# First stage of a two-layer trunk written as an explicit in-order pipeline on four queues

## The chip, the cores and the metric

The kernel runs on 1 core of one Trainium2 chip. The metric is the device time of one execution in microseconds (us), taken as the median of the runs of a kernel. Below, PE is TensorE, DVE is VectorE, ACT is ScalarE, POOL is GpSimd, and SP is SyncE, whose queue issues nearly all transfers.

## The reference

One sequence of 512 tokens with model width 2048 goes through two layers. Layer 0 is forgetting attention (32 heads of 64), layer 1 is RWKV-7 time mixing; each sits under a normalisation whose shift and scale come from a second input `c`, and ends in a gated residual addition. Everything is float32. What matters here is the head of layer 0:

```python
c_act = jax.nn.silu(c)                                  # (1, 2048)
mod = c_act @ w_mod[i] + b_mod[i]                       # 3 * 2048 outputs
shift, scale, gate = jnp.split(mod, 3, axis=-1)
h = rms_norm(x, norm_w[i]) * (1.0 + scale) + shift      # (512, 2048)
# layer 0:
proj = h @ w_in                                         # 2048 -> 4 * 2048 + 32
q, k, v, z, f_logit = ...                               # parts of proj
out = (softmax(q k / 8 + cum_t - cum_s) v * silu(z)) @ w_out
```

## The kernel before

Activations are held transposed, as 16 tiles of 128 channels by 512 tokens (`KT = 16`). A product in float32 quality is made of three matmuls on operands cut into a high and a low half (`mm3`): high weight by high activation, low weight by high activation, high weight by low activation. So each weight tile is loaded (`raw`), copied by ACT into its high half (`whi`), and DVE subtracts to get the low half (`wlo`). Activations are cut likewise (`hi`, `lo`).

The first stage (the block `with tc.tile_pool(name="st0"...)`, from line 397) does this. The tiles of x are loaded, squared and summed over channels on PE (`ss`); from that comes the reciprocal root `rstd`. `cb` is silu(c) spread over all partitions. `mod_unit` makes shift or scale for one channel tile: it loads a 128 x 2048 tile of w_mod in two halves (`wm`, 512 KB each), DVE multiplies each by `cb` and sums along the row into one column of `mraw`, and POOL adds the two columns and the bias (for scale also multiplies by the norm weight). Then, for each k of 16: the stage's weights `wst0` (672 columns: forget gates and q, k, v of the first heads) are loaded and cut; `xn` is x by `rstd` on POOL (DVE for k = 0), shift and scale are put on by ACT, the result is cut into `A[k]`; and six products go into six PSUM banks (`tr`, `pv`, `ss`, `tr`, `S`, `S`), each accumulated over the 16 k. After k = 3, 7 and 11 come nine blocks of the gate projection z (`NZ = 9`): for each of nine output tiles a 256 KB weight tile is loaded and cut, twelve matmuls run into one of two `pj` banks, ACT copies the bank to `zt`, and POOL adds it to `zs` (the first time ACT writes `zs` itself). The last quarter of these nine tiles is made later (`zfin`).

All of this stage's program order on each engine is chosen by a scheduler from the dependences. Buffers come in rings: three `wm`, three `raw`, four `whi`, four `wlo`; a load waits until the ring's oldest tile has had its last reader. SP takes its transfers strictly in order.

After the stage the order is written out by a planner (`Flow` and `backbone`): a list of weight tiles is multiplied in a fixed row on PE, with the side work of attention (normalisation of q and k in `norm`, scores, transposes) placed in between at planned times. `InOrder.on` forces each engine to keep the order in which instructions are written; it is switched on there for PE, ACT and DVE. The first four weight tiles are fetched and cut ahead of the first product, then `first()` starts the side work: ACT copies k of the first heads out of PSUM, squares q for its norm, and so on.

Of the kernel before, what the change touches and what calls it, by code (L numbers as in the profile page):

```python
# [17 lines left out]
P = 128  # L18
T = 512
# [110 lines left out]
def body(ctx, tc, a, out, dbg=None, stop=0):  # L130
# [258 lines left out]
    with ExitStack() as s0:  # L389
# [7 lines left out]
        with tc.tile_pool(name="st0", bufs=2, reuse_waits="tile") as q:  # L397
            xs = []
            cb, cs, i = silu_c(cbp)
            s0.enter_context(table("natural_log_exp_and_others", i))  # L400
            for k in range(KT):
                x = q.tile([P, T], F, tag=f"r{k}", name=f"x{k}", bufs=1)
                sp.dma_start(x, a["xT"][k])
                xs.append(x)
            ss = bank("ss")
            for k in range(KT):
                sq = q.tile([P, T], F, tag=("sq", "sq", "xn", "zt")[k % 4], name="sq",
                            bufs=4 - k % 4 // 2 * 2)
                if k < 5:
# [3 lines left out]
                if k % 2:  # L413
                    dve.tensor_tensor(out=sq, in0=old, in1=sq, op=OP.add)
                    pe.matmul(ss, onesD, sq, start=k == 1, stop=k == KT - 1)
                if k % 2 and k < 8:
                    o = bank("tr")
                    for i in range(4):
                        n = k // 2 * 4 + i
                        pe.matmul(o[:, i * P:(i + 1) * P], cs[:, n:n + 1].broadcast_to([P, P]),  # L420
                                  ident, start=True, stop=True)
                    act.activation(cb[:, k // 2 * T:(k // 2 + 1) * T], o, AF.Copy)
                old = sq
            rstd = rstd_of(q, ss, eps, 1e-6, "rs0", bufs=1)
            st = [bank(t) for t in ("tr", "pv", "ss", "tr", "S", "S")]
            cols = [(0, P)] + [(32 + i * P, 32 + (i + 1) * P) for i in range(5)]
            for k in range(KT):
                for part in (1, 0):
                    for _ in mod_unit(q, cb, 0, part, k):
                        pass  # L430
                w = wload(a["wst0"][k:k + 1].rearrange("k p n -> p k n"), 1, NS0, "s", q)
                xn = q.tile([P, T], F, tag="xn", name="xn")
                (pool if k else dve).tensor_tensor(out=xn, in0=xs[k], in1=rstd, op=OP.mult)
                act.activation(xn, xn, AF.Identity, scale=scale[:, 0, k:k + 1],
                               bias=shift[:, 0, k:k + 1])
                A.append(new_act(k))
                split(A[k][0], A[k][1], xn)
                for o, (m0, m1) in zip(st, cols):
                    mm3(o[0:m1 - m0, :], w, 0, A[k], k == 0, k == KT - 1, m0, m1)
                if k % WK < WK - 1 or k == KT - 1:  # L440
                    continue
                k0 = k - WK + 1
                for j in range(NZ):
                    w = wload(a["wz"][j][:, k0:k + 1, :], WK, P)
                    o = bank("pj")
                    for i in range(WK):
                        mm3(o, w, i, A[k0 + i], i == 0, i == WK - 1)
                    if k0 == 0:
                        act.activation(zs[j], o, AF.Copy)
# [258 lines left out]
        def gatings():  # L708
            while len(odone) < KT or len(mdone) < 12 * KT:
# [905 lines left out]
```

## Time and profile before

| | |
|---|---|
| median of 3 runs | 2509.62 us (2505.53 to 2510.38) |
| the profiled execution | 2509.14 us |
| its span, first to last instruction | 2507.4 us |
| mean granted PE clock | 0.973 |
| PE busy | 2350.3 us, 94%, 13620 matmuls |
| DVE busy | 1659.4 us, 66% |
| ACT busy | 1251.2 us, 50% |
| POOL busy | 864.4 us, 34% |
| transfers | 476.08 MB, mean 190 GB/s |

A busy share is an average over stages with different limits. In the table of 40 slices the PE row begins `6878999`, so the first slices, about 62.7 us each, are less full than most others. All helpers record their operations under one line (L88), so instructions are told apart by the names of their tiles. A matmul's recorded duration is longer than its distance to the next one, since matmuls overlap; the distance is the pace.

### The profile page before, as it was taken

How to read it: one execution, taken by the hardware profiler on the slowest of the kernel's cores; microseconds unless marked ns; L12 is line 12 of the kernel's file. 1: busy time of each engine (PE TensorE's matmuls, PEld its weight loads, DVE VectorE, ACT ScalarE, POOL GpSimd, SP SyncE). 2: the span in 40 equal slices, each digit the busy share in tenths (PEclk: the TensorE clock that was granted, in tenths of full speed). 3: DMA queues.
4: the chain of work that ended last, by engine and by line, in shares of the span. 5: the costliest groups of instructions: out<-in, count | busy, mean ns of one | idle time of the engine just before them, and what ended most of it. 6: DMA issues, size and time to landing. Idle time of an engine off the chain costs nothing. (4 is left out here: it accounts for less than half of the span.)

```text
span 2507.4 us, 40113 instructions
## 1 busy us (share of the span) xinstructions
PE 2350.3 (94%) x13620; PEld 1818.3 (73%) x13620; DVE 1659.4 (66%) x3143; ACT 1251.2 (50%) x2300; POOL 864.4 (34%) x1280
## 2 busy tenths in 40 slices
PE   6878999999999999996999998997999999999999
PEld 4666777877777788884766676776677767777787
DVE  6776878888887545339696666662567877776332
ACT  3335655555565544226447775742344545555321
POOL 4464533433333100117341239731334444442000
PEclk8989999999999999998999998998999999999999
DMA  8765666666664264445656886776756656554443
GB/s 277 259 236 174 213 208 202 214 207 209 208 212 153 93 230 164 144 135 184 205 168 230 279 250 206 224 212 193 195 159 176 191 157 179 161 149 149 147 147 97
DMA packets 343582, 476.08 MB, mean 190 GB/s; under 512 B 146768, under 2 KB 157136, under 8 KB 343376
## 3 DMA queue, kind: packets, MB, share of 16 engines
q1 hardware_dynamic: 341712, 470.88, 60.5%
q0 software_dynamic: 1664, 2.63, 0.3%
q8 instruction: 108, 1.77, 0.3%
q14 instruction: 98, 0.80, 0.1%
HBM read 377.42 MB, written 95.95 MB: 189 GB/s over the span
## 5 line engine op out<-in xcount | busy, mean ns | idle before, releaser
L88 PE MATMUL pj<-hi,whi 128*128 128x512 f32 x2416 | 995.4, 412 | 31.1 <-ACT zt L88 13.1
L88 PE MATMUL pj<-hi,wlo 128*128 128x512 f32 x2416 | 958.3, 397 | 14.0 <-DVE wlo L88 13.9
L88 PE MATMUL pj<-lo,whi 128*128 128x512 f32 x2416 | 957.7, 396 | 2.3 <-DVE lo L88 2.3
L88 DVE TENSOR_TENSOR wlo<-raw,whi 128x512 fp32r<-128x512 f32 (+2 forms) x628 | 488.0, 785 | 288.9 <-ACT whi L88 284.9
L88 ACT ACTIVATE whi<-raw 128x512 fp32r<-128x512 f32 (+2 forms) x628 | 394.0, 634 | 421.9 <-PE pj L88 229.5
L88 PEld LDWEIGHTS pj<-hi,whi 128*128 128x128 f32 x2416 | 459.8, 190 | 139.5 <-ACT zt L88 15.7
L88 PEld LDWEIGHTS pj<-lo,whi 128*128 128x128 f32 x2416 | 459.6, 190 | 106.2 <-DVE lo L88 3.4
L88 PEld LDWEIGHTS pj<-hi,wlo 128*128 128x128 f32 x2416 | 460.9, 191 | 102.5 <-DVE wlo L88 18.4
L88 DVE CUSTOM_DVE_ANT_0 wm<-wm,cb 128x1024 f32<-128x1024 f32 x192 | 245.4, 1285 | 23.7 <-DMA wm<-in_wmodT 23.5
L88 POOL TENSOR_SCALAR SV<-SV,dec 64x64 f32<-64x64 f32 x224 | 92.4, 413 | 220.1 <-DVE SV L88 205.7
L88 POOL TENSOR_SCALAR mx<-mx 128x1 f32<-128x1 f32 x128 | 64.8, 507 | 144.3 <-DVE mx L88 96.6
L88 ACT ACTIVATE pr<-Sm,mx 128x128 f32<-128x128 f32 (+3 forms) x128 | 71.5, 559 | 80.2 <-POOL mx L88 80.1
L88 POOL TENSOR_SCALAR pr<-pr,rc 128x128 f32<-128x128 f32 (+3 forms) x128 | 97.0, 758 | 22.6 <-DVE rc L88 18.4
L88 DVE COPY SV<-x 64x64 f32<-64x64 f32 x256 | 56.7, 222 | 62.7 <-PE x L88 55.6
L88 DVE CUSTOM_DVE_ANT_0 Sm<-S,cmask 128x128 f32<-128x128 f32 (+3 forms) x128 | 62.1, 485 | 34.6 <-PE S L88 33.7
L88 POOL TENSOR_TENSOR lt<-lane 128x30 f32<-128x30 f32 (+14 forms) x90 | 61.9, 687 | 64.3 <-DMA lane<-mld 57.5
L88 POOL TENSOR_TENSOR acc<-acc,sq 128x512 f32<-128x512 f32 x14 | 18.2, 1297 | 161.5 <-ACT sq L88 161.5
L88 DVE TENSOR_TENSOR SV<-SV,x 64x64 f32<-64x64 f32 x224 | 49.0, 219 | 37.5 <-PE x L88 31.9
L88 POOL TENSOR_SCALAR scale<-mraw,bsc 128x1 f32<-128x1 f32 x32 | 39.8, 1244 | 97.9 <-DVE mraw L88 96.6
L88 POOL TENSOR_TENSOR lane<-lane,lt 128x30 f32<-128x30 f32 (+14 forms) x90 | 63.6, 706 | 7.0
L88 POOL TENSOR_TENSOR bk<-bk,eI 128x512 f32<-128x512 f32 x32 | 36.8, 1151 | 79.4 <-PE S L88 53.4
L88 PE MATMUL S<-k,q 128*128 128x128 f32 (+7 forms) x256 | 62.4, 325 | 0.0
(316 smaller groups left out, 3478.3 us busy)
## 6 DMA issues: line engine op xcount, KB each, us to landing
wm<-in_wmodT SPq DMA_DIRECT2D x192, 512.0 KB, 4.5
raw<-in_wz SPq DMA_DIRECT2D x128, 256.0 KB, 3.8
raw<-in_wo SPq DMA_DIRECT2D x128, 256.0 KB, 3.6
raw<-in_wv SPq DMA_DIRECT2D x124, 256.0 KB, 3.7
raw<-in_wk SPq DMA_DIRECT2D x96, 256.0 KB, 3.6
raw<-in_wr SPq DMA_DIRECT2D x64, 256.0 KB, 4.6
raw<-in_wq SPq DMA_DIRECT2D x56, 256.0 KB, 3.9
mxd<-m SPq DMA_DIRECT2D x48, 256.0 KB, 3.0
```

The costliest lines, as they stand in the source:

```text
L88: self.last = f(*a, **k)
```

## The change

The four queues PE, ACT, DVE and SP are switched to the written order for the first stage, and the stage is written out as a pipeline in that order.

- w_mod tiles are loaded whole (1 MB; only the first two in halves), three in the ring, and `mod0` reduces one with a single instruction. The bias is the start value of the sum, and the result is written to `shift` or `scale` directly. The norm weight enters in the operation that makes `xn`. POOL does nothing in the stage.
- The squares of the first six x tiles go to `ss` singly instead of in pairs; `cb` is made before the squares that ACT does.
- The products of z are spread over the steps: `z_unit` is one k of one z tile (three matmuls). For k below 4 two tiles advance by one unit per step; later a step has 7 units (k below 8) or 9 between the products of the stage's own columns. Weights of z are loaded four tiles ahead (`z_load`) and cut two ahead (`z_split`).
- ACT copies the first quarter of each z tile out of PSUM as before; the additions of the second and third are done by DVE straight from PSUM (`zadds`).
- In step k the operand of step k + 1 is made after the first third of the products, and two w_mod tiles are reduced after the second and the last third.
- The condition in `gatings` counts 8 KT instead of 12 KT reductions, because `mod0` does not enter its reductions in `mdone`.

```diff
-            for k in range(KT):
+            for e in (pe, act, dve, sp):
+                e.on = True
...
+            def mod0(n, parts=1):
+                if n >= 2 * KT:
+                    return
+                k, part, w, m = n // 2, 1 - n % 2, wms[n], D // parts
+                acc = (bsc[:, 0, k:k + 1] if part else vecs[:, V_BM, k:k + 1])
+                for i in range(parts):
+                    s = slice(i * m, (i + 1) * m)
+                    o = (scale if part else shift)[:, 0, k:k + 1] if i == parts - 1 else \
+                        mraw[:, part, i:i + 1]
+                    dve.tensor_tensor_reduce(out=w[:, s], in0=w[:, s], in1=cb[:, s], scale=1.0,
+                                             scalar=acc, op0=OP.mult, op1=OP.add, accum_out=o)
+                    acc = o
...
+            def operand(k):
+
+                if k >= KT:
+                    return
+                xn = q.tile([P, T], F, tag="xn", name="xn")
+                dve.scalar_tensor_tensor(out=xn, in0=xs[k], scalar=vecs[:, V_NW, k:k + 1],
+                                         in1=rstd, op0=OP.mult, op1=OP.mult)
+                act.activation(xn, xn, AF.Identity, scale=scale[:, 0, k:k + 1],
+                               bias=shift[:, 0, k:k + 1])
+                A.append(new_act(k))
+                act_hi(A[k][0], xn)
+                dve.tensor_tensor(out=ws[k][1], in0=rws[k], in1=ws[k][0], op=OP.subtract)
+                zadds()
+                dve.tensor_tensor(out=A[k][1], in0=xn, in1=A[k][0], op=OP.subtract)
...
+            def z_unit(n, i):
+                j, g = zt[n]
+                if i == 0:
+                    zo[n] = bank("pj")
+                mm3(zo[n], zw[n], i, A[g * WK + i], i == 0, i == WK - 1)
+                if i == WK - 1:
+                    zend.append(n)
+
+            def zadds():
+                while zend:
+                    n = zend.pop(0)
+                    j, g = zt[n]
+                    if g == 0:
+                        act.activation(zs[j], zo.pop(n), AF.Copy)
+                    else:
+                        dve.tensor_tensor(out=zs[j], in0=zs[j], in1=zo.pop(n), op=OP.add)
...
+                if k == 11:
+                    mod0(0, 2)
...
+            mod0(1, 2)
...
+            w_hi(0)
+            operand(0)
+            w_load(1)
+            wm_load(3)
+            wm_load(4)
+            for n in range(2):
+                z_split(n)
+            mod0(2)
+            mod0(3)
...
             for k in range(KT):
-                for part in (1, 0):
-                    for _ in mod_unit(q, cb, 0, part, k):
-                        pass
...
+                w_hi(k + 1)
+                for part in range(3):
+                    for o, (m0, m1) in list(zip(st, cols))[2 * part:2 * part + 2]:
+                        mm3(o[0:m1 - m0, :], ws[k], 0, A[k], k == 0, k == KT - 1, m0, m1)
+                    if k < WK:
+                        if part:
+                            z_unit(part - 1, k)
                     else:
-                        z = q.tile([P, T], F, tag="zt", name="zt")
-                        act.activation(z, o, AF.Copy)
-                        pool.tensor_tensor(out=zs[j], in0=zs[j], in1=z, op=OP.add)
+                        for n in range(nz, nz + (2 + (part == 1) if k < 2 * WK else 3)):
+                            z_unit(n // WK, n % WK)
+                            if n % WK == 0:
+                                z_split(n // WK + 2)
+                                z_load(n // WK + 4)
+                            nz += 1
+                    if part == 0:
+                        operand(k + 1)
+                        w_load(k + 2)
+                    else:
+                        zadds()
+                        mod0(2 * k + 3 + part)
+                        wm_load(2 * k + 4 + part)
...
+            zadds()
+            for e in (pe, act, dve, sp):
+                e.on = False
...
-            while len(odone) < KT or len(mdone) < 12 * KT:
+            while len(odone) < KT or len(mdone) < 8 * KT:
```

The order of instructions after this stage is the same in both kernels on all five engines. Inside it, three places are shown, as the engine's queue has them in program order (numbers are those of the buffers, and each program numbers its own).

DVE before, between the low halves of two neighbouring operands late in the stage (`wlo` is a split of weights, `wm` with `mraw` a half reduction, `lo` the low half of an activation):

```order
L88 TENSOR_TENSOR lo_1097<-xn_1093,hi_1096 128x512
L88 TENSOR_TENSOR wlo_1007<-raw_1004,whi_1006 128x512
L88 ISA wm_1121,mraw_89<-wm_1121,cb_158 128x1024
L88 ISA mraw_89 128x1
L88 ISA wm_1126,mraw_89<-wm_1126,cb_158 128x1024
L88 ISA mraw_89 128x1
L88 ISA wm_1129,mraw_89<-wm_1129,cb_158 128x1024
L88 ISA mraw_89 128x1
L88 ISA wm_1164,mraw_89<-wm_1164,cb_158 128x1024
L88 ISA mraw_89 128x1
L88 TENSOR_TENSOR lo_1143<-xn_1139,hi_1142 128x512
```

DVE now, at a like place (step 9 to the operand of step 10):

```order
L88 TENSOR_TENSOR zs0_146<-zs0_146,pj_814 128x512
L88 ISA wm_803,scale_91<-wm_803,cb_158,bsc_86 128x2048
L88 ISA scale_91 128x1
L88 TENSOR_TENSOR wlo_883<-raw_822,whi_882 128x512
L88 TENSOR_TENSOR zs1_147<-zs1_147,pj_849 128x512
L88 ISA wm_864,shift_90<-wm_864,cb_158,vecs_63 128x2048
L88 ISA shift_90 128x1
L88 SCALAR_TENSOR_TENSOR xn_910<-x10_185,vecs_63,rs0_283 128x512
L88 TENSOR_TENSOR wlo_894<-raw_838,whi_892 128x672
L88 TENSOR_TENSOR zs2_148<-zs2_148,pj_878 128x512
L88 TENSOR_TENSOR lo_914<-xn_910,hi_913 128x512
```

Four half reductions became two whole ones; `xn` and the additions to `zs` came from POOL, and each addition reads a `pj` bank that PE must have finished.

PE before, where the z block after k = 3 begins (`S` holds the stage's own columns of k = 3, `pj` is a z tile):

```order
L88 MATMUL S_279<-hi_442,whi_435 128x512
L88 MATMUL S_279<-hi_442,wlo_436 128x512
L88 MATMUL S_279<-lo_443,whi_435 128x512
L88 MATMUL pj_470<-hi_304,wlo_467 128x512
L88 MATMUL pj_470<-lo_305,whi_466 128x512
L88 MATMUL pj_470<-hi_350,whi_466 128x512
L88 MATMUL pj_470<-hi_350,wlo_467 128x512
L88 MATMUL pj_470<-lo_351,whi_466 128x512
```

PE now, in step 4 after its first three matmuls:

```order
L88 MATMUL pv_320<-hi_472,whi_460 128x512
L88 MATMUL pv_320<-hi_472,wlo_462 128x512
L88 MATMUL pv_320<-lo_473,whi_460 128x512
L88 MATMUL pj_526<-hi_298,whi_505 128x512
L88 MATMUL pj_526<-hi_298,wlo_506 128x512
L88 MATMUL pj_526<-lo_299,whi_505 128x512
L88 MATMUL pj_526<-hi_337,whi_505 128x512
L88 MATMUL pj_526<-hi_337,wlo_506 128x512
L88 MATMUL pj_526<-lo_338,whi_505 128x512
L88 MATMUL ss_321<-hi_472,whi_460 128x512
```

and on DVE the split that this z tile needs, `wlo_506`, in its row:

```order
L88 TENSOR_TENSOR lo_473<-xn_469,hi_472 128x512
L88 ISA wm_454,scale_91<-wm_454,cb_158,bsc_86 128x2048
L88 ISA scale_91 128x1
L88 ISA wm_490,shift_90<-wm_490,cb_158,vecs_63 128x2048
L88 ISA shift_90 128x1
L88 TENSOR_TENSOR wlo_506<-raw_456,whi_505 128x512
L88 TENSOR_TENSOR wlo_510<-raw_458,whi_509 128x512
```

A z tile stood in one piece of twelve matmuls and now stands in pieces between the columns of a step; two whole reductions stand ahead of its low half.

DVE before, at the end of the stage (`wlo_1604` to `wlo_1622` are the four weight tiles of the part that follows, `l_1642` the first norm's low half):

```order
L88 TENSOR_TENSOR lo_1571<-xn_1567,hi_1570 128x512
L88 TENSOR_TENSOR wlo_1604<-raw_1601,whi_1603 128x512
L88 TENSOR_TENSOR wlo_1610<-raw_1607,whi_1609 128x512
L88 TENSOR_TENSOR wlo_1616<-raw_1613,whi_1615 128x512
L88 TENSOR_TENSOR wlo_1622<-raw_1619,whi_1621 128x512
L88 TENSOR_TENSOR wlo_1518<-raw_1515,whi_1517 128x672
L88 TENSOR_TENSOR wlo_1564<-raw_1561,whi_1563 128x672
L88 TENSOR_TENSOR l_1642<-sq_1630,h_1641 128x512
```

DVE now (`wlo_1428` to `wlo_1446` are those four, `zs8` takes the last z tile):

```order
L88 TENSOR_TENSOR zs6_152<-zs6_152,pj_1352 128x512
L88 TENSOR_TENSOR zs7_153<-zs7_153,pj_1375 128x512
L88 TENSOR_TENSOR zs8_154<-zs8_154,pj_1394 128x512
L88 TENSOR_TENSOR wlo_1428<-raw_1425,whi_1427 128x512
L88 TENSOR_TENSOR wlo_1434<-raw_1431,whi_1433 128x512
L88 TENSOR_TENSOR wlo_1440<-raw_1437,whi_1439 128x512
L88 TENSOR_TENSOR wlo_1446<-raw_1443,whi_1445 128x512
L88 TENSOR_TENSOR l_1466<-sq_1454,h_1465 128x512
```

The four splits stood ahead of the stage's last two weight tiles; they now stand behind the addition of the last z tile, which reads the stage's last product.

## Rows read from the trace of the kernel before

**Rows 1.** Windows: span, busy us of each engine, granted clock, DMA share, GB/s
```profile
30.80:220.07 189.27, 158.24 (x612) 123.28 (x613) 129.82 (x178) 64.33 (x107) 100.20 (x80) 0.92 0.70 236
220.07:2507.40 2287.33, 2178.64 (x12961) 1686.89 (x12959) 1509.53 (x2935) 1172.13 (x2169) 754.42 (x1173) 0.98 0.60 185
```

**Rows 2.** Waits from 30.8 to 220.07: who for whom, us, times, longest
```profile
ACT xn L88 <- POOL shift L88: 60.5, 14, 8.3
...
DVE wm L88 <- DMA wm<-in_wmodT: 22.4, 17, 2.3
...
PE tr L88 <- ACT hi L88: 13.2, 2, 10.4
PE pj L88 <- ACT zt L88: 13.1, 5, 3.5
```

**Rows 3.** Groups by shape, 30.8 to 220: busy us, mean ns, idle before
```profile
L88 DVE CUSTOM_DVE_ANT_0 wm<-wm,cb 128x1024 f32<-128x1024 f32 x58 | 80.2, 1401 | 22.4 <-DMA wm<-in_wmodT 22.4
...
L88 DVE TENSOR_TENSOR wlo<-raw,whi 128x512 fp32r<-128x512 f32 x31 | 28.5, 925 | 9.0 <-ACT whi L88 8.8
```

**Rows 4.** Timeline, 195 to 206: start us, us, instruction, idle before it
```profile
195.68 0.50 PE L88 MATMUL pj<-hi,whi 128*128 128x512 f32 x1 [3.28 <-ACT zt L88]
195.71 1.30 POOL L88 TENSOR_TENSOR zs<-zs,zt 128x512 f32<-128x512 f32 x1 [2.08 <-ACT zt L88]
195.78 2.31 DVE L88 CUSTOM_DVE_ANT_0 wm<-wm,cb 128x1024 f32<-128x1024 f32 x1
...
198.02 1.22 DVE L88 CUSTOM_DVE_ANT_0 wm<-wm,cb 128x1024 f32<-128x1024 f32 x1
...
198.98 0.63 PE L88 MATMUL pj<-hi,whi 128*128 128x512 f32 x1
...
199.16 1.22 DVE L88 CUSTOM_DVE_ANT_0 wm<-wm,cb 128x1024 f32<-128x1024 f32 x1
...
199.41 0.63 PE L88 MATMUL pj<-hi,wlo 128*128 128x512 f32 x1
...
205.29 0.69 DVE L88 TENSOR_TENSOR lo<-xn,hi 128x512 fp32r<-128x512 f32 x1 [4.90 <-ACT hi L88]
...
205.90 0.68 DVE L88 TENSOR_TENSOR wlo<-raw,whi 128x512 fp32r<-128x512 f32 x1
```

**Rows 5.** The chain that ended last, its last piece: start us, us, what
```profile
2345.01 158.49 PE pj L88 x690
```

**Rows 6.** Timeline, 16 to 31
```profile
16.81 3.60 PE L88 MATMUL ss<-sq,onesD 128*128 128x512 f32 x8
...
28.48 0.68 DVE L88 TENSOR_TENSOR xn<-x,rs 128x512 f32<-128x512 f32 x1
...
30.78 0.80 PE L88 MATMUL tr<-hi,whi 128*128 128x512 f32 x1 [10.38 <-ACT hi L88]
```

**Rows 7.** DMA issues, 30.8 to 200: count, KB each, median us to landing
```profile
wm<-in_wmodT SPq DMA_DIRECT2D x55, 512.0 KB, 5.1
raw<-in_wz SPq DMA_DIRECT2D x30, 256.0 KB, 4.3
```

**Rows 8.** Windows of two shorter stretches, columns as in rows 1
```profile
60.00:97.70 37.70, 34.79 (x150) 27.79 (x149) 26.65 (x40) 13.96 (x23) 16.41 (x14) 1.00 0.83 276
95.00:100.00 5.00, 2.52 (x11) 1.73 (x11) 2.00 (x3) 0.93 (x2) 1.36 (x3) 1.00 0.98 357
```

**Rows 9.** Timeline, 218 to 232.6, where the in-order part begins
```profile
218.21 0.60 ACT L88 ACTIVATE k<-ss 128x512 f32<-128x512 f32 x1 [5.99 <-PE ss L88]
...
220.07 0.39 PE L88 MATMUL pj<-hi,whi 128*128 128x512 f32 x1
...
220.47 0.69 DVE L88 TENSOR_TENSOR l<-sq,h 128x512 fp32r<-128x512 f32 x1 [7.35 <-ACT h L88]
...
223.74 0.39 PE L88 MATMUL ss<-l,blkr 128*128 128x512 f32 x1
...
232.15 0.50 PE L88 MATMUL ss<-l,blkr 128*128 128x512 f32 x1 [1.00 <-DVE l L88]
```

More of the change, by code (lines that the diff above doesn't have):

```diff
@@ new lines, in body, with z_load, z_split @@
+            zt = [(j, 0) for j in range(NZ)] + [(j, g) for g in (1, 2) for j in range(NZ)]
+            zraw, zw, zo, zend = {}, {}, {}, []
+            def z_load(n):
+                if n < len(zt):
+                    j, g = zt[n]
+                    zraw[n] = wp.tile([P, WK, P], F, tag="raw", name="raw", bufs=3)
+                    sp.dma_start(zraw[n], a["wz"][j][:, g * WK:g * WK + WK, :])
+            def z_split(n):
+                if n < len(zt):
+                    hi = wp.tile([P, WK, P], R, tag="whi", name="whi")
+                    lo = wp.tile([P, WK, P], R, tag="wlo", name="wlo")
+                    split(hi, lo, zraw.pop(n))
+                    zw[n] = hi, lo
@@ new lines, in body @@
+            cb, cs, i = silu_c(cbp)
+            s0.enter_context(table("natural_log_exp_and_others", i))
+            for k in range(8):
+                xload(k)
+            wm_load(0, 2)
+            for k in range(8, KT):
+                xload(k)
+            wm_load(1, 2)
+            w_load(0)
+            wm_load(2)
+            for n in range(2):
+                z_load(n)
+            for i in range(4):
+                o = bank("tr")
+                for n in range(4 * i, 4 * i + 4):
+                    pe.matmul(o[:, n % 4 * P:(n % 4 + 1) * P],
+                              cs[:, n:n + 1].broadcast_to([P, P]), ident, start=True, stop=True)
+                act.activation(cb[:, i * T:(i + 1) * T], o, AF.Copy)
@@ L412, in body @@
                     act.activation(sq, xs[k], AF.Square)
-                if k % 2:
+                if k < 6:
+                    pe.matmul(ss, onesD, sq, start=k == 0, stop=False)
+                elif k % 2:
                     dve.tensor_tensor(out=sq, in0=old, in1=sq, op=OP.add)
[L415 to L422, printed above, removed]
@@ L423, in body @@
-                old = sq
-            rstd = rstd_of(q, ss, eps, 1e-6, "rs0", bufs=1)
+                    pe.matmul(ss, onesD, sq, start=False, stop=k == KT - 1)
+                old = sq
+                if k == 11:
+                    mod0(0, 2)
+            rstd = q.tile([P, T], F, tag="rs0", name="rs0", bufs=1)
+            act.activation(rstd, ss, AF.Ln, bias=eps)
+            act.activation(rstd, rstd, AF.Exp, scale=-0.5)
+            mod0(1, 2)
+            u = q.tile([P, T], F, tag="sq", name="rs0u")
@@ L432, in body @@
[L432 to L439, printed above, removed]
@@ L455, in body @@
+                if k == WK - 2:
+                    for n in (2, 3):
+                        z_load(n)
+                if k == WK - 1:
+                    z_split(2)
+                    z_split(3)
+                    z_load(4)
+                    z_load(5)
+                ws.pop(k)
+            zadds()
+            for e in (pe, act, dve, sp):
+                e.on = False
         fl = Flow()
```

49 lines of the change are left out of this document (32 added, 17 removed).

## The prediction, made before the changed kernel was run

> **What bounds the kernel now.** I read the stages first [rows 1]: from 30.80, when the first product of the first stage starts, to 220.07, when the first product of the long in-order part starts, TensorE runs the stage's 612 matmuls in 189.27 us and is busy for 158.24 of them. The last piece of the chain of waits gives the pace at full clock: 690 matmuls in 158.49 us [rows 5], 0.230 us each, so 612 would be 141 us. So 48 us of this stretch are no work: 31 idle, the rest matmuls 0.43 us apart (198.98 to 199.41) at the lower clock, after a wait of 3.28 at 195.68 [rows 4]. Then I read who waits [rows 2]. ACT stands 60.5 us before its normalisation for POOL's `shift`, in 14 of 15 steps, and POOL stands behind VectorE's reductions; TensorE's own waits are for `hi`, whose source that normalisation is, and for the copies `zt` out of the two `pj` banks. No engine is full: the stage is a relay through POOL. VectorE is stretched as well: reductions `wm` average 1401 ns and 512-wide splits 925 [rows 3], where undisturbed ones take 1.22 and 0.68 [rows 4]; the 2.31 us one at 195.78 lies beside a POOL addition at 195.71.
>
> After the stage TensorE is busy for 2178.64 of 2287.33 us [rows 1], and the instruction order there is the same before and after on all five engines, so a shift of that part's start should reach the end nearly whole. The profiled execution took 2509.14 us (span 2507.4 and 1.7 around it), 0.5 below the median 2509.62 of the three runs; the sum goes against it.
>
> The Trainium skill (SBUF — State Buffer, the section on door types and the shared port) says that VectorE, with two SBUF inputs, and GpSimd take one port pair from each other for a whole instruction. The stretched reduction agrees. By that rule all VectorE work in the new stage runs at its undisturbed times, as I take it; without it, at 1401 ns per half, the ten reductions on the path below would cost 5.5 us more.
>
> **The change, part by part.** *The start* (to the first product, 30.78 now). Removed from the path: five reductions of 1.14 (198.02 to 199.16 [rows 4]) stand on VectorE between the squares and the operand, and some load waits. Added: four half reductions there, 4.6, three more double matmuls into `ss` (11 instead of 8 at 2 x 0.45, from 3.60 us for 8 singles [rows 6]), 2.7, and the sixteen small matmuls that spread c, now ahead of all squares. These cancel to about 1: I take 31.0, bounds 29.5 (ACT hides the additions) to 34 (nothing hides).
>
> *Durations.* A 2048-wide reduction replaces two 1024-wide ones and their two accumulator reads; above it is 2 x 1.14 = 2.28, below it saves one read and one start, about 2.2. I take 2.25. POOL's two or three small operations per step go to nothing, since the bias enters as the reduction's start value and the norm weight in the xn operation. From VectorE's xn to the first product is 30.78 - 28.48 = 2.30 [rows 6], with the wider split inside; the low half adds 0.61 (205.29 to 205.90 [rows 4]). So an operand costs VectorE 2.9.
>
> *Step 0 to 4.* After the first operand come its low half, two splits of z weights (0.61 each), two reductions and the next operand: 0.6 + 1.2 + 4.5 + 2.3 = 8.6, so step 1 starts at 39.6. TensorE's 24 matmuls (12 cold at 0.43, 12 at 0.23: 7.9) fit under it. Steps 1 to 3 are VectorE's: two reductions and an operand, 7.4 each against 24 x 0.23 = 5.5 for TensorE. Step 4 starts at 61.8.
>
> *A new wait in step 4.* VectorE's queue holds the split of z tile 2 behind the two reductions of step 3, so it is ready 0.6 + 4.5 + 0.6 = 5.7 after step 4 starts, and TensorE asks for it after 7 matmuls, 1.6. It stands 4.1 us, with everything of that step behind it, and by the matmuls from 195.68 to 199.41 [rows 4] a wait near 3.3 is followed by a cold spell; 12 matmuls at 0.20 extra are 2.4. Bounds 0 (VectorE ahead) to 6.5; I take 6.5.
>
> *Steps 4 to 15.* TensorE: 4 x 39 x 0.23 = 35.9 and 8 x 45 x 0.23 = 82.8. VectorE per step: 4.5 + 2.9 + 1.75 splits, 8.5 against 9.0; later 4.5 + 2.9 + 2.25 splits + 2.25 additions to z (0.61 to 0.69, one of them inside the operand's wait), 9.6 against 10.35. TensorE is late last, by little; cover that is gone would cost VectorE's excess directly. z additions that moved from POOL now stand in VectorE's queue and wait for TensorE; behind them are the step's reductions, but the next operand is needed a step later, which leaves some 4 us. End of the stage: 61.8 + 6.5 + 35.9 + 82.8 = 187.0.
>
> *Loads.* The bytes stay: 32 MB of w_mod, 16 x 336 KB, 27 x 256 KB, 16 x 256 KB of x, together 50.3 million bytes; issues get fewer, since 30 w_mod tiles now come whole instead of in halves. About 10.8 million can be in by 36 us (three w_mod tiles are the limit). The remaining 38.9 up to the last reduction must be in by 171.5 (two steps less an operand and a reduction before the end), 287 GB/s. The fullest long stretch now has 276 at a share of 0.83, a short one 357 at 0.98 [rows 8], so at full share it fits. I price it at 0; the upper bound is the second rival.
>
> *The handoff.* Now ACT copies k at 218.21, before the stage ends, because the four weight tiles are split; the second norm product is then ready when TensorE comes to it: its low half starts at 220.47 and ends at 221.16, the product comes at 223.74, 2.6 later [rows 9]. In the new order the first two weight splits stand on VectorE behind the last z addition (0.2 + 0.61 + 0.61 = 1.4 after the end), and the fourth tile's load needs the first one's buffer: 1.4 + 4.3 [rows 7] + 0.5 for ACT's split puts the k copy at +6.2 instead of -1.9. From that copy to TensorE's second norm pair at 232.15 are 13.9 us, 11.3 without the slack; it comes at +17.5 instead of +12.1. Cost 5.5; bounds 1.4 (only the split) to 8 (no slack used).
>
> **Sum.** 220.07 - 187.0 - 5.5 = 27.6 gained: 2509.14 - 27.6, about 2482.
>
> **Rivals.** *(a) The loads become the bound.* At 256 GB/s, between the stage's 236 [rows 1] and 276, 38.9 million bytes take 152 us, arrive at 188 instead of 171.5, and the stage ends 16.5 later: 2498. For it: VectorE waits 22.4 us for `wm` now [rows 2]. Against: those are waits on 512 KB pieces in three small buffers, while three tiles of 1 MB now hold twice as much ahead.
>
> *(b) The cold clock spreads.* VectorE-bound steps leave TensorE idle 1.9 us of 7.4. If it stays at 1.2 GHz there, a step needs 24 x 0.43 = 10.3 instead of 7.4: three steps cost 8.7, 2491. Against: the 5 us at 95 have 2.48 us of idleness and a granted clock of 1.00 [rows 8]. [...]
>
> *(c) Slower: one load at a time.* SP's queue is in order, and a w_mod load can stand behind a z-weight load that waits for VectorE's split, which stands behind a reduction that waits for w_mod. If no two such loads overlap, each costs 5.1 [rows 7] for its first half and 1.5 for the second at 357 GB/s, 6.6. The 28 loads from the fifth on then end at 36 + 185 = 221, the stage near 241, and the kernel at 2536. It decides from about 5.6 us per load. Against: load n waits only for reduction n - 3.
>
> *(d) No change.* The gain is lost in the attention part, if VectorE and ACT bound that and not TensorE: 2507 to 2511. Against it is TensorE's share there.
>
> **Numbers.** Forecast 0.66, (a) 0.16, (b) 0.08, (c) 0.06, (d) 0.04. Forecast's own range: start 1.5 early, no wait in step 4, handoff 3 gives 2471; start 3 late, VectorE 5.5 more, handoff 8 gives 2493. With most of (a) in, the range is 2470 to 2500. Faster by over 0.2% (5 us, about what can be told from no change): 0.88; same 0.06; slower 0.06.
>
> **What would show it.** Right: 612 matmuls of the stage within 156 us; no POOL operation in it; reductions of 2.25; first product near 31; a wait of about 4 us in step 4 for a z split; the k copy on ACT about 6 us after the stage's last product, and a wait before the first norm product. Wrong: VectorE's waits for `wm` above 30 us (a), clock under 0.9 between 40 and 62 (b), steps of 13 us from step 8 on (c), or an equal gain in the stage that the end does not show (d).

## The result, and the profile after

The changed kernel takes 2490.13 us (median of 4 runs, 2487.10 to 2492.47) beside 2510.00 for the kernel before: ratio 0.9921, 95% interval 0.9901 to 0.9941, 19.9 us faster. The prediction was 2482, its range 2470 to 2500. The profiled execution took 2492.47 us, its span is 2490.6.

The same two stretches as in [rows 1], with the same columns: from the first product to the first product of the in-order part, and from there to the end.

```profile
32.39:189.59 157.20, 148.52 (x613) 117.99 (x613) 128.59 (x150) 53.67 (x84) 0.76 (x2) 0.96 0.73 265
189.59:2490.60 2301.01, 2188.05 (x12961) 1695.07 (x12959) 1512.86 (x2940) 1174.22 (x2173) 751.73 (x1173) 0.97 0.60 184
```

The stage is 32.1 us shorter (157.20 instead of 189.27), POOL is out of it (0.76 instead of 100.20), and the stretch behind it is 13.7 us longer. The stage ends 30.5 us earlier (189.59 instead of 220.07), and more than a third of that is given back behind it.

Who waits for whom from 30.8 to 220.07, as in [rows 2]:

```profile
ACT xn L88 <- DVE xn L88: 59.5, 16, 5.5
...
ACT whi L88 <- DMA raw<-in_wz: 11.6, 2, 8.2
PE tr L88 <- ACT hi L88: 10.8, 5, 6.0
...
PE pj L88 <- DVE wlo L88: 5.1, 2, 3.9
```

ACT's 60.5 us for POOL's `shift` are gone, but it now waits 59.5 for VectorE's xn. So the sum of ACT's waits does not say what the stage loses; TensorE's waits do, and they are few and nearly all lie before step 5. VectorE by shape, 30.8 to 190, as in [rows 3]:

```profile
L88 DVE CUSTOM_DVE_ANT_0 wm<-wm,cb,vecs 128x2048 f32<-128x2048 f32 x15 | 35.2, 2348 | 2.0 <-DMA wm<-in_wmodT 1.9
...
L88 DVE TENSOR_TENSOR wlo<-raw,whi 128x512 fp32r<-128x512 f32 x27 | 18.4, 688 | 2.0 <-ACT whi L88 2.0
```

A whole reduction takes 2.35 us where two halves took 2 x 1.40, a split 0.69 where it took 0.93, and VectorE waits for w_mod 1.9 us where it waited 22.4.

TensorE in step 4 (timeline; start, length, idle before):

```profile
63.37 0.51 PE L88 MATMUL tr<-hi,whi 128*128 128x512 f32 x1 [1.40 <-ACT hi L88]
...
69.44 0.80 PE L88 MATMUL pj<-hi,wlo 128*128 128x512 f32 x1 [3.92 <-DVE wlo L88]
70.04 0.63 PE L88 MATMUL pj<-lo,whi 128*128 128x512 f32 x1
70.47 0.63 PE L88 MATMUL pj<-hi,whi 128*128 128x512 f32 x1
...
74.31 0.61 PE L88 MATMUL pj<-hi,whi 128*128 128x512 f32 x1
74.73 0.42 PE L88 MATMUL pj<-hi,wlo 128*128 128x512 f32 x1
74.99 0.40 PE L88 MATMUL pj<-lo,whi 128*128 128x512 f32 x1
```

Step 4 begins at 63.37, TensorE stands 3.92 us for the low half of z tile 2, and the matmuls that follow are 0.43 apart until 74.7: the granted clock is 0.50 from 70 to 74.7, the lower of its two levels. The handoff, as in [rows 9]:

```profile
189.79 0.69 DVE L88 TENSOR_TENSOR zs<-zs,pj 128x512 f32<-128x512 f32 x1 [3.43 <-PE pj L88]
190.39 1.89 DVE L88 TENSOR_TENSOR wlo<-raw,whi 128x512 fp32r<-128x512 f32 x3
...
194.51 0.63 ACT L88 ACTIVATE whi<-raw 128x512 fp32r<-128x512 f32 x1 [8.21 <-DMA raw<-in_wz]
195.04 0.58 ACT L88 ACTIVATE k<-ss 128x512 f32<-128x512 f32 x1
...
197.23 0.49 PE L88 MATMUL ss<-h,blkr 128*128 128x512 f32 x1 [2.61 <-ACT h L88]
...
199.15 0.68 DVE L88 SCALAR_TENSOR_TENSOR l<-u,e 32x512 f32<-32x512 f32 x1 [1.24 <-ACT e L88]
199.67 1.29 POOL L88 TENSOR_TENSOR zs<-zs,zt 128x512 f32<-128x512 f32 x1 [37.11 <-ACT zt L88]
199.93 2.11 DVE L88 TENSOR_TENSOR_SCAN on<-on,l 32x512 f32<-32x512 f32 x1
...
209.03 0.67 DVE L88 TENSOR_TENSOR l<-sq,h 128x512 fp32r<-128x512 f32 x1
...
209.75 0.79 PE L88 MATMUL ss<-l,blkr 128*128 128x512 f32 x1 [2.99 <-DVE l L88]
...
228.30 0.78 PE L88 MATMUL ss<-l,blkr 128*128 128x512 f32 x1 [1.08 <-DVE l L88]
```

ACT stands 8.21 us for the fourth weight tile, whose load needed the first tile's buffer, and that tile's split stands on VectorE behind the last z addition; the copy of k comes 5.45 after the stage's end. The second norm pair ends its wait at +20.16 (209.75 - 189.59); before it was +12.08. The third pair is at +38.71; before it was at +28.53. VectorE's way to the second pair and the third pair itself, in the kernel before:

```profile
222.34 0.68 DVE L88 SCALAR_TENSOR_TENSOR l<-u,e 32x512 f32<-32x512 f32 x1 [1.18 <-ACT e L88]
223.12 1.21 DVE L88 TENSOR_TENSOR_SCAN on<-on,l 32x512 f32<-32x512 f32 x1
...
231.43 0.67 DVE L88 TENSOR_TENSOR l<-sq,h 128x512 fp32r<-128x512 f32 x1
...
248.60 0.50 PE L88 MATMUL ss<-l,blkr 128*128 128x512 f32 x1 [1.10 <-DVE l L88]
```

From there the distance between the two traces, counted product by product, is 19.8 us and stays so for 1400 us. Around 1640 the profiled run loses three more: a transfer (`lane<-mld`) lands later, and TensorE waits 2.15 us for a `wlo` at 1643.48. In the traces of most other kernels here the distance to the kernel before shrinks by 2 to 4 us at that place too. The difference of the medians is 19.9.

### The profile page after: what moved, and what is told of

The parts are those of the page before. It is cut to its first block, busy times and chain, and to the rows that moved or that the text cites. A ratio compares the mean times of both kernels' runs of the same rounds, so it can differ in the third digit from the quotient of the medians.

```text
span 2490.6 us, 39903 instructions
## 1 busy us (share of the span) xinstructions
PE 2353.3 (94%) x13626; PEld 1822.1 (73%) x13626; DVE 1657.5 (67%) x3114; ACT 1244.2 (50%) x2282; POOL 757.5 (30%) x1199
## 5 line engine op out<-in xcount | busy, mean ns | idle before, releaser
L88 PE MATMUL pj<-hi,wlo 128*128 128x512 f32 x2416 | 960.0, 397 | 20.2 <-DVE wlo L88 20.1
L88 DVE TENSOR_TENSOR wlo<-raw,whi 128x512 fp32r<-128x512 f32 (+2 forms) x628 | 476.8, 766 | 280.2 <-ACT whi L88 277.4
L88 DVE CUSTOM_DVE_ANT_0 wm<-wm,cb 128x1024 f32<-128x1024 f32 x128 | 157.7, 1232 | 0.2
L88 POOL TENSOR_SCALAR pr<-pr,rc 128x128 f32<-128x128 f32 (+3 forms) x128 | 96.6, 755 | 22.4 <-DVE rc L88 18.6
L88 PE MATMUL tr<-ident,pr 128*128 128x128 f32 x320 | 56.4, 274 | 4.1 <-DVE pT L88 2.8
```

Of the source, the lines that this page charges most:

```text
L88: self.last = f(*a, **k)
```

## Experiments

All edits are to the changed kernel. "Scheduler" means that the order in the stage is left to the scheduler; "POOL" that POOL stands between VectorE and ACT; "length" is from the first product to the first product of the in-order part; "pair 2" is the second norm pair, counted from there. First product, length and pair 2 are of the profiled execution, "time" is the median. Ratios are to the kernel before as it ran in the same batch, where its median lay between 2507.1 and 2510.1; medians of different batches can differ by that much. So below, small differences are read from the traces: from the third norm pair on, the distance of each trace to that of the kernel before stays the same to about 0.2 us for 600 us.

| run | order | POOL | z written | first product | length | pair 2 | time | ratio, 95% |
|---|---|---|---|---|---|---|---|---|
| before | scheduler | yes | blocks | 30.78 | 189.3 | +12.1 | 2510.0 | |
| changed | written | no | spread | 32.39 | 157.2 | +20.2 | 2490.1 | 0.9921 (0.9901 to 0.9941) |
| split_early | written | no | spread | 32.39 | 152.8 | +20.2 | 2486.2 | 0.9923 (0.9900 to 0.9946) |
| handoff | written | no | spread | 31.56 | 156.1 | +14.1 | 2482.9 | 0.9905 (0.9884 to 0.9927) |
| start | written | no | spread | 31.40 | 156.9 | +20.3 | 2488.3 | 0.9926 (0.9899 to 0.9952) |
| mended | written | no | spread | 32.05 | 158.3 | +14.1 | 2479.1 | 0.9885 (0.9865 to 0.9905) |
| z_pool | written | for z only | spread | 32.50 | 160.5 | +20.1 | 2492.0 | one run |
| pool_mods | written | yes | spread | 30.97 | 168.0 | +20.2 | 2499.5 | 0.9957 (0.9942 to 0.9972) |
| z_block | written | no | blocks | 32.49 | 185.3 | +15.3 | 2514.6 | 1.0021 (1.0011 to 1.0031) |
| free_order | scheduler | no | spread | 35.57 | 143.7 | +20.3 | 2476.8 | 0.9886 (0.9864 to 0.9907) |
| free_pool | scheduler | yes | spread | 35.43 | 161.4 | +20.3 | 2493.0 | 0.9934 (0.9914 to 0.9954) |
| free_block | scheduler | no | blocks | 32.65 | 144.5 | +12.2 | 2466.4 | 0.9825 (0.9800 to 0.9849) |
| free_handoff | scheduler | no | spread | 34.70 | 144.3 | +14.1 | 2468.6 | 0.9834 (0.9817 to 0.9850) |
| free_handoff_z | scheduler | no | spread | 32.38 | 144.9 | +12.7 | 2466.0 | 0.9831 (0.9814 to 0.9848) |

**split_early.**

```diff
                         operand(k + 1)
                         w_load(k + 2)
+                        if k == WK - 1:
+                            z_split(2)
+                            z_split(3)
...
-                if k == WK - 2:
+                if k == 0:
                     for n in (2, 3):
                         z_load(n)
                 if k == WK - 1:
-                    z_split(2)
-                    z_split(3)
```

> The low halves of z tiles 2 and 3 are made on VectorE ahead of the two reductions of step 3 instead of behind them (their loads are issued three steps earlier). Theory A: TensorE's wait of 3.92 us in step 4 and the 12 matmuls at 0.43 instead of 0.23 after it (2.4) are pure loss, since VectorE has slack from step 4 on: the wait goes, the stage ends 6 us earlier (183.5 instead of 189.59), the kernel takes about 2484. Theory B: VectorE is what bounds steps 4 to 7, and the wait only shows it early: the idle time comes back a step later, the stage ends within 1.5 us of 189.6 and the time stays at 2489 to 2491.

The wait of 3.92 and the cold spell are gone and the stage is 4.4 shorter, not 6. TensorE's waits from 60 to 190:

```profile
PE pj L88 <- ACT zs L88: 1.5, 1, 1.5
PE pj L88 <- DVE wlo L88: 1.2, 1, 1.2
```

The first row is new: 1.5 for ACT's copy of a z tile; the second stands at 186.75, behind the stage's end (185.20). The end lies nearer to A's 183.5 than to B: the wait in step 4 was loss, less what came back. The ratios (0.9923 against 0.9921) do not separate the two kernels. The traces do, by 4.1 us at the third norm pair.

**handoff.**

```diff
+    own = [1]
...
-        for n in range(4):
+        for n in range(4 - len(own)):
             for _ in fetch(n):
                 pass
+        if own:
+            fl.start(0, fetch(3))
+        own.clear()
```

> The fourth weight tile of the in-order part is fetched by a planned task like the later ones, so ACT's copy of k no longer stands behind a split that waits for a transfer. Theory A: the handoff costs 8 us because ACT waits 8.2 for that load. Then the k copy comes about 3 before the stage's last product instead of 5.4 after it, the second norm pair comes at +12 to +13 instead of +20.2, the third is 7 to 8 earlier, and the kernel takes about 2483. Theory B: what holds the second pair is VectorE, stretched beside POOL's additions to zs (a scan of 2.11, a split of 1.77): the second pair stays at +17 or later, the gain is under 3 us, time 2487 to 2490.

TensorE's norm products (timeline):

```profile
192.57 0.39 PE L88 MATMUL ss<-h,blkr 128*128 128x512 f32 x1
...
200.18 0.49 PE L88 MATMUL ss<-h,blkr 128*128 128x512 f32 x1 [1.72 <-ACT h L88]
201.82 0.50 PE L88 MATMUL ss<-l,blkr 128*128 128x512 f32 x1 [1.14 <-DVE l L88]
```

The k copy comes at 184.32, 3.4 before the stage's end (187.70), the first pair waits for nothing, the second is at +14.1, the third at +32.1: 6.6 of the 10.2 are back. A holds, with a rest of 3.6. Its 7 us in the medians come from different batches; by the ratios it is 4, by the traces 8.5.

**start.**

```diff
-                if k == 11:
-                    mod0(0, 2)
+                if k in (7, 9):
+                    mod0(0, 2, (k - 7) // 2)
```

The third argument, new in `mod0`, picks one of the two halves.

> The two half reductions of the first scale tile move from between VectorE's additions of squares (19.8 to 22.3) into its waits after the additions of x7 and x9. Theory A: they stand on the path to rstd, so the sum of squares ends 1.5 to 2.5 earlier and the first product comes at 29.0 to 30.5 instead of 32.39; time 2487 to 2488. Theory B: the w_mod tile has not landed by 17 us, or the later loads set the early steps: the first product within 0.5 of 32.4, or it is earlier and step 4 starts at 63 as now; time 2490.

First product at 31.40, 1.0 earlier; that lies between A and B, and the run `handoff`, whose start is unchanged, has 31.56. This one is inconclusive.

**free_order.**

```diff
-            for e in (pe, act, dve, sp):
-                e.on = True
             xs, wms = [], []
```

> The stage is written as in the changed kernel, but the order on TensorE, ACT, VectorE and the load queue is left to the scheduler. Theory A (the written order is what counts): the stage ends at 205 to 220 and the time goes back to 2500 to 2510. Theory B (taking POOL out of the chain and spreading the z products is what counts, whoever sets the order): the stage ends within 6 us of 189.6 and the time is 2484 to 2496.

A is out, and the gain is larger than B allows: the time is under B's lower edge. The same instructions in the scheduler's order make a stage of 143.7 us, in which TensorE is never idle. Behind the handoff this trace is 11.8 us ahead of the changed kernel's, though its first product comes 3.2 later (by the ratios 8.8 us). VectorE around the operand of step 1, in the changed kernel and then here (timelines):

```profile
38.73 0.75 DVE L88 SCALAR_TENSOR_TENSOR xn<-x,vecs,rs 128x512 f32<-128x512 f32 x1
39.39 0.85 DVE L88 TENSOR_TENSOR wlo<-raw,whi 128x672 fp32r<-128x672 f32 x1
41.02 0.69 DVE L88 TENSOR_TENSOR lo<-xn,hi 128x512 fp32r<-128x512 f32 x1 [0.78 <-ACT hi L88]
41.63 2.35 DVE L88 CUSTOM_DVE_ANT_0 wm<-wm,cb,bsc 128x2048 f32<-128x2048 f32 x1
```

```profile
36.80 0.74 DVE L88 SCALAR_TENSOR_TENSOR xn<-x,vecs,rs 128x512 f32<-128x512 f32 x1
37.46 2.34 DVE L88 CUSTOM_DVE_ANT_0 wm<-wm,cb,bsc 128x2048 f32<-128x2048 f32 x1
...
39.73 0.68 DVE L88 TENSOR_TENSOR lo<-xn,hi 128x512 fp32r<-128x512 f32 x1
```

The scheduler puts a reduction between xn and the low half, so VectorE works while ACT makes the high half; from 36 to 61 its row shows no wait. Operand 1 follows operand 0 after 3.5 us instead of 8.6, and step 4 does not wait. The wait of 0.78 is the smaller part of that difference: in the scheduler's row both z splits (30.09, 31.29), the next weight split (32.49) and a reduction (27.21) are done ahead of the first low half, before and among the operations that make `rstd`, and in the written row they stand behind it. Of the 13.5 us of length, 6.8 lie in steps 0 to 3 (31.0 against 24.1) and 6.6 behind them, where step 4's wait and cold spell alone made 6.0.

**pool_mods.** `mod0` reduces halves into `mraw` again, POOL adds them, and:

```diff
-                dve.scalar_tensor_tensor(out=xn, in0=xs[k], scalar=vecs[:, V_NW, k:k + 1],
-                                         in1=rstd, op0=OP.mult, op1=OP.mult)
+                (pool if k else dve).tensor_tensor(out=xn, in0=xs[k], in1=rstd, op=OP.mult)
```

> The written order stays, but POOL is put back between VectorE and ACT: each w_mod tile is reduced in two halves, POOL adds halves and bias (and multiplies the scale by the norm weight), and POOL makes xn for all tiles but the first. Theory A (the relay through POOL is what the old stage paid for): ACT waits for POOL in nearly every step again, the stage ends at 205 or later instead of 189.59, time 2500 or more. Theory B (the relay cost what it did because each reduction stood right before its use; in the written order shift and scale are made a step ahead): ACT's waits for POOL's shift stay under 10 us in total, the stage ends between 187 and 196, time 2487 to 2496.

Between the two: the in-order part starts at 198.95, 9.4 later. Waits from 32 to 215:

```profile
ACT xn L88 <- POOL shift L88: 94.2, 15, 7.6
...
DVE lo L88 <- ACT hi L88: 26.4, 15, 2.3
```

ACT waits for POOL in every step, as A has it, but at a lower price than A's: VectorE waits 26.4 us where it waited 9.3, and steps 1 to 3 take 9.4 instead of 7.44. The additions to zs stay on VectorE in this run.

**z_block.** `z_unit`, `z_split` and `zadds` stand in a loop over the nine tiles after steps 3, 7 and 11, and the loads of z move with them:

```diff
+                if k % WK == WK - 1 and k < KT - 1:
+                    g = k // WK
+                    for j in range(NZ):
+                        n = g * NZ + j
...
```

> The written order stays, but the products of z stand in three blocks of nine tiles after steps 3, 7 and 11 again, not spread; reductions stay two to a step. Theory A (spreading counts): 11 steps without z are VectorE's at 7.44 each, three steps with a block are TensorE's at 126 x 0.23 = 29, the last is 4.1; from step 1 at 41.0 the stage ends near 214, 24 later than now, time about 2513. Theory B (spreading is worth little, POOL's absence made the gain): the stage ends before 198, time under 2499.

A: the in-order part starts at 217.74, 28 later, and the kernel is 0.2% slower than before the change. In this written order the spreading is needed.

**z_pool.**

```diff
-                        dve.tensor_tensor(out=zs[j], in0=zs[j], in1=zo.pop(n), op=OP.add)
+                        z = lq.tile([P, T], F, tag="og", name="zt")
+                        act.activation(z, zo.pop(n), AF.Copy)
+                        pool.tensor_tensor(out=zs[j], in0=zs[j], in1=z, op=OP.add)
```

> The 18 additions to zs go by way of ACT (copy) and POOL as in the old kernel; all else is as in the changed one. Theory A: a POOL addition holds up a VectorE instruction beside it, so some of the 30 whole reductions take over 3 us instead of 2.27 and their mean rises to about 2.7, while the end of the stage moves less than 3 us, since TensorE is full there. Theory B: the two engines don't disturb each other, the mean stays under 2.35, and VectorE is freed of 12 us of additions.

VectorE and POOL (their timelines, put in order of time):

```profile
149.93 2.34 DVE L88 CUSTOM_DVE_ANT_0 wm<-wm,cb,vecs 128x2048 f32<-128x2048 f32 x1
150.00 3.41 POOL L88 TENSOR_TENSOR zs<-zs,zt 128x512 f32<-128x512 f32 x1 [2.15 <-ACT zt L88]
...
157.23 1.39 POOL L88 TENSOR_TENSOR zs<-zs,zt 128x512 f32<-128x512 f32 x1 [3.82 <-ACT zt L88]
157.39 3.38 DVE L88 CUSTOM_DVE_ANT_0 wm<-wm,cb,bsc 128x2048 f32<-128x2048 f32 x1
```

A in kind, with both sizes off. Who pays is decided by who starts first: where the addition is first (157.23) the reduction takes 3.38 instead of 2.34; where the reduction is first (149.93) it keeps its 2.34, and the addition takes 3.41 instead of 1.3. The mean of the 30 reductions is 2.48, less than the 2.7 expected, and the stage ends 3.4 later, more than expected. This agrees with what the Trainium skill (SBUF — State Buffer, section "SBUF: two separate sides") says of the port pair that VectorE and GpSimd share: whichever starts first holds it for the whole instruction, and the other waits.

**free_handoff.** Both edits, `free_order` and `handoff`.

> Order in the stage left to the scheduler, and the fourth weight tile of the in-order part fetched by a planned task. Theory A: the two gains are of different places and add up: stage end near 179 as with the scheduler's order, the second norm pair at about +14 instead of +20, time about 2470. Theory B: with the scheduler's order the loads or VectorE at the end of the stage hold the handoff anyway: second pair at +18 or later, time 2474 to 2477.

A: the gains add up. Second pair at +14.1, 2468.6.

**free_pool.** Both edits, `free_order` and `pool_mods`.

> Order in the stage left to the scheduler, z products spread, but POOL back between VectorE and ACT (half reductions, bias and xn on POOL). Theory A: POOL in the chain costs about as much as under the written order (9.4): stage end 187 to 191 instead of 179.3, time about 2486. Theory B: the scheduler hides it by running reductions ahead: stage end within 3 of 179.3, time 2475 to 2479. Theory C: POOL in the chain is what made the old stage slow, spreading did little: stage end 205 or later, time above 2500.

The length grows by 17.7 (161.4), more than A's 9.4; with the first product where `free_order` has it, the in-order part starts at 196.79, between A and C. The scheduler cannot hide POOL. VectorE's half reductions, from 40 to 190 (as in [rows 3]):

```profile
L88 DVE CUSTOM_DVE_ANT_0 wm<-wm,cb 128x1024 f32<-128x1024 f32 x55 | 70.3, 1307 | 0.0
```

C fails too, and that matters for the whole account: with POOL back in the chain ACT waits 59.3 us for its `shift`, about as in [rows 2], yet the stage is 27.9 us shorter than before. In this run VectorE no longer waits for w_mod (22.4 before), and TensorE's 13.1 for `zt` are gone, since VectorE adds z straight from PSUM.

**free_block.** Both edits, `free_order` and `z_block`.

> Order in the stage left to the scheduler, POOL out of the chain, z products written in three blocks after steps 3, 7 and 11. Theory A: without spreading TensorE runs dry between the blocks whatever sets the order: stage end 203 to 209 (28 after 179.3, as under the written order), time about 2505. Theory B: the scheduler spreads or runs VectorE ahead by itself: stage end before 190, time under 2488.

B: length 144.5, TensorE busy for all of it. The scheduler moves the z products between the steps by itself. And it has the z tiles done earlier, so nothing of z stands at the stage's end (TensorE's norm products, timeline):

```profile
180.86 0.39 PE L88 MATMUL ss<-l,blkr 128*128 128x512 f32 x1
...
189.28 0.50 PE L88 MATMUL ss<-l,blkr 128*128 128x512 f32 x1 [1.06 <-DVE l L88]
```

From 177.12 that is +12.2, as before the change, with no edit of the handoff.

**mended.** `split_early`, `start` and `handoff` together, and in steps 1 to 3:

```diff
+                            xn_dve(k + 1)
+                            xn_act(k + 1)
...
                         mod0(2 * k + 3 + part)
+                        if part == 1 and 0 < k < WK:
+                            low(k + 1)
```

> The written order with four places changed: splits of z tiles 2 and 3 ahead of the reductions of step 3, the first scale reductions in the waits of the squares, in steps 0 to 3 a reduction between xn and the low halves (so that VectorE does not wait 0.77 for ACT), and the fourth weight tile of the in-order part fetched by a planned task. Theory A (the written order lost its 10 us against the scheduler's only at these places): first product 31.4, steps 1 to 3 of 6.7 instead of 7.44, step 4 at 61, stage end about 182.5, second norm pair at +14, time about 2477. Theory B (the row itself is dearer, in steps 4 to 15 too): stage end at 186 or later, time 2481 or more.

The stage ends at 190.37, as B has it, but not by B's reason, and the time is between A's and B's. VectorE in step 3, and TensorE's second product of step 4 (timelines):

```profile
61.04 0.75 DVE L88 SCALAR_TENSOR_TENSOR xn<-x,vecs,rs 128x512 f32<-128x512 f32 x1
63.86 1.29 DVE L88 TENSOR_TENSOR wlo<-raw,whi 128x512 fp32r<-128x512 f32 x2 [2.07 <-ACT whi L88]
65.07 2.34 DVE L88 CUSTOM_DVE_ANT_0 wm<-wm,cb,bsc 128x2048 f32<-128x2048 f32 x1
...
67.34 0.85 DVE L88 TENSOR_TENSOR wlo<-raw,whi 128x672 fp32r<-128x672 f32 x1
68.11 0.68 DVE L88 TENSOR_TENSOR lo<-xn,hi 128x512 fp32r<-128x512 f32 x1
68.25 0.79 PE L88 MATMUL tr<-hi,wlo 128*128 128x512 f32 x1 [4.39 <-DVE wlo L88]
```

The z splits now wait 2.07 for ACT, and the weight split and the low half of step 4's operand stand behind them and a reduction: 68.1 instead of 63.4. TensorE, which stood 3.92 for a z tile, now stands 4.39 for that weight split. The stage is no shorter (158.3), and by the traces the run gains no more than `handoff` does. Whether the four places were all that the written order lost is not shown by it.

**free_handoff_z.** `free_handoff`, and the last addition to zs behind the first three low halves:

```diff
+            fl.start(0, fetch(3))
+            zadds()
...
-                        zadds()
+                        if k < KT - 1 or part < 2:
+                            zadds()
...
-            zadds()
```

> As the scheduler's order with the planned fetch (2468.6), and the last addition to zs written behind the low halves of the first three weight tiles of the in-order part. Theory A: TensorE's wait of 1.2 for the first low half goes and the later chain follows: second norm pair at +12 to +13, time 2465 to 2467. Theory B: the chain on ACT sets the second pair: it stays at +14, time 2467 to 2470.

Pair 2 at +12.7, the third at +29.1 (before: +28.5), so the rest of the handoff is gone. 2466.0 against 2468.6 is not told apart by the medians. It and `free_block` are the fastest, some 23 us below the changed kernel.

## Why the prediction was right, and what it missed

- *First product at 31.0*: 32.39, within its bounds. The net cost that I took as small was 1.4 more.
- *Step 1 at 39.6, steps 1 to 3 of 7.4*: step 1 at 41.04, steps of 7.44. VectorE sets them as worked out. (612 matmuls within 156 us were foretold; it is 157.2.) I counted the 0.77 in which VectorE waits for ACT as part of the operand, and all that VectorE does in a step as standing in its row; `free_order` shows that both are a matter of order.
- *A wait of 4.1 and a cold spell of 2.4 in step 4*: 3.92, and 2.1 (69.44 to 74.31 for 12 matmuls, less 12 x 0.23). The granted clock, 0.50 from 70 to 74.7, is the lower level. That it fell behind the wait of 3.92 agrees with the Trainium skill (TensorE: Matmul & The Clock Gate, section "Why this matters for your kernels"), which warns of long gaps between bursts of matmuls. The idle 1.3 to 1.4 us at the steps before were not followed by it.
- *Steps 4 to 15*: step 8 begins at 106.44, 43.1 after step 4 (6.5 + 35.9 = 42.4 predicted); the rest takes 83.15 (82.8 predicted). End at 189.59 instead of 187.0.
- *POOL out, reductions 2.25, no VectorE work stretched*: 2.27 from one to the next, splits 0.69, in place of 2 x 1.40 and 0.93. `z_pool` shows the stretch come back.
- *The stage is a relay through POOL*: true of who waits for whom, but not of the price. ACT waits some 60 us for its operand in stages of 189.3 (for POOL), 161.4 (`free_pool`, for POOL) and 157.2 us (for VectorE).
- *Loads priced at 0*: VectorE waits 1.9 us for w_mod. Rival (a) did not come, nor (c); (b) neither: between 40 and 60 the granted clock is 1.00. (c)'s figures don't come out of the terms that it names: from load ends at 221 the same step as in the sum (171.5 to 187.0) leads to 236.5, not 241, and 135.5 us for 28 loads are 4.8 each, not 5.6.
- *The handoff, 5.5, at most 8*: this step failed by size. The k copy came at +5.45 (6.2 predicted), by the wait that I named. But it cost 8.1 at the second norm pair and 10.2 at the third, 10.7 by the constant distance of 19.8 behind it (30.5 gained at the stage's end). What I had wrong is the slack. From the k copy to the second pair I took 11.3, the 13.9 of before less 2.6 of slack, and it was 14.7. The 2.6 are slack on the way through TensorE's first norm product, and the second pair does not hang on that way: it hangs on VectorE's row, which waits for ACT's `e` and then runs almost without a gap to the pair's low half. That way took 4.1 + 9.1 + 0.7 us before (copy at 218.21, 222.34, 231.43, 232.15) and 4.1 + 9.9 + 0.7 now (195.04, 199.15, 209.03, 209.75), so it had no slack to give; the 0.8 is the net of what instructions beside POOL's additions grew (the scan from 1.21 to 2.11). And I followed the delay no further than the second pair. TensorE's wait of 2.99 there is followed by a granted clock of 0.50 from 210 to 214, which is about the 2.1 us that the third pair loses on top. `handoff` gives 6.6 back and `free_handoff_z` nearly all the rest, so the pieces are the fourth load in ACT's row and the last z addition in VectorE's.

The stage is 2.6 later than predicted and the handoff 5.2 dearer: 27.6 - 7.8 = 19.8, which is the measured difference. The handoff lies above its own bound of 8; that the time is still in the range is owed to the room left for terms that did not come, the loads above all.

What the prediction did not ask is which part makes the gain. Neither the written order nor the spreading by hand is needed for it: `free_block` has neither, its stage is 44.8 us shorter than before, and it loses nothing in the handoff. That is 43 us of gain, where the changed kernel has 20. The two differ by 12.5 us at the stage's end and by the handoff's 10.7. The written order costs 13.5 us of length (157.2 against 143.7, the same code), and without the spreading far more (`z_block`, 185.3 against 144.5). The spreading saves 0.8 us of length under the scheduler (143.7 against 144.5) and puts a z tile at the stage's end, which costs `free_order` 9 us in the handoff.

What in the rest of the rewrite makes the 43 is shown only in part. Putting POOL back for shift, scale and xn, with the half reductions that go with it, costs 17.7 us of length under the scheduler (`free_pool`) and 10.8 under the written order (`pool_mods`). The other 27.9 of the 44.8 lie between the kernel before and `free_pool`, and are open. In between, the additions to zs went from POOL to VectorE, w_mod got whole loads and so a ring of twice the bytes, loads and operands are written a step ahead, the squares are summed singly, and z is spread. A run with this code under the scheduler, with POOL in the chain and z in blocks, would tell whether the spreading is worth something while POOL is in; it was not made.

The first product varies by 3 us between runs with the same instructions ahead of it (35.57, 34.70 and 32.38 in the three with the scheduler's order, spread z and no POOL), and the traces show why. TensorE's sums of squares in `free_order` and in `free_handoff_z` (timelines):

```profile
15.93 8.06 PE L88 MATMUL ss<-sq,onesD 128*128 128x512 f32 x10 [2.72 <-DVE sq L88]
```

```profile
14.92 2.84 PE L88 MATMUL ss<-sq,onesD 128*128 128x512 f32 x6 [2.04 <-DVE sq L88]
```

In the first, the half reduction ahead of the squares gets its w_mod tile 1.0 us later (it starts at 12.56 instead of 11.54), and behind the longer wait the granted clock is 0.53 from 15 to 20 instead of 1.00: 0.81 us a matmul instead of 0.47. Of the 11.3 us between the traces of `free_order` and `free_block` 2.9 are this kind of luck at the start and 9 are the handoff, less 0.8 of length.

## What to carry to other kernels

Before writing an order by hand, run the rewritten code with the scheduler's order: a written row has to beat that with the same instructions, and here it did not. When several things change at once, put them back one by one and with each other's absence in mind; POOL's share here is 17.7 or 10.8 us of a stage depending on who sets the order, and no sum of waits told it. Price the end of a stage not by its last product but by what stands on each queue behind it. Slack found on one way into an instruction counts only if no other way is as long, so follow each engine's row to it, and carry a delay through to the place from which the distance to the old trace is constant.

## What the runs showed of the hardware

Beside each other, a POOL addition of 128x512 and a VectorE reduction of 128x2048 do not share the cost (`z_pool`): the one that starts second takes about 1 to 2 us more (reduction 3.38 instead of 2.34, addition 3.41 instead of 1.3), the first keeps its time.

TensorE ran 144.9 us of products with no idle time (`free_handoff_z`) while loads moved 276 GB/s, so loads were no limit at this pace either.

TensorE's granted clock fell to its lower level behind waits of 3.92 us (changed kernel, step 4) and 2.72 us (`free_order`, at 15.93), and stayed at 1.00 behind 2.04 (`free_handoff_z`, at 14.92). The wait alone does not decide it: two waits of 0.97 and 1.08 us before the third norm pair are followed by 0.59 from 228 to 230 in the changed kernel, and in the kernel before two of 0.97 and 1.10 at the same pair are followed by 1.00 from 248 to 252.
